# Add-residual RMSNorm: 64 KiB runs in three fixed slots, all transfers in one queue

## The chip, the cores and the metric

The kernel runs on one core of one Trainium2 chip. The metric is the device time of one execution in microseconds (us), as the median of several runs. Beside it there is one profiled execution, from which all durations of single instructions and transfers come.

## The reference

```python
def reference(x, residual, gamma, eps):
    z = x + residual
    rms = np.sqrt(np.mean(z ** 2, axis=-1, keepdims=True) + eps)
    return (z / rms * gamma).astype(np.float32)
```

The arrays x, residual and the output are 32 x 2048 x 2048 in float32, so 65,536 rows of 2,048 elements, 537 MB each. gamma has 2,048 elements. Each row is added, its mean square is taken, and the row is scaled by one number and by gamma. There is no matrix product. Each element of x and residual is read once, and each of the output is written once: 1,611 MB pass between HBM and SBUF, the memory on the core.

## The kernel before, in words

SBUF has 128 partitions. The rows are cut into 256 tiles of 256 rows; in each tile a partition holds R = 2 neighbouring rows (L29), so that its part of a transfer is one run of 16 KiB, and a transfer moves 2 MiB.

One loop (L50) runs over the tiles. For each it loads x (L53) and residual (L54) through SyncE's DMA queue (SP, queue q1 of the profile). VectorE (DVE) adds the two in place into the x tile, both rows in one instruction (L56). ScalarE (ACT) squares each row and sums it in the same instruction (L61), the squares themselves going to a scratch tile in PSUM that nobody reads; then it takes the root of mean plus eps (L69). VectorE forms the reciprocal (L77), and scales each row by it and by gamma in one instruction, again in place (L80). ScalarE's own queue then stores the x tile to the output (L89; queue q10).

What orders the work are the tile pools, from which the framework sets the waits: six buffers for x (L45) and four for residual (L46). A load of x waits until the store that used its buffer six tiles earlier has landed; a load of residual waits until the add that read its buffer has ended. Instructions of one engine, DMA issues among them, go in the order of the program, so a DMA issue that waits holds all that are behind it in the same queue.

gamma is brought to all partitions by one DMA ahead of the loop that reads its 8 KiB 128 times (L41).

Of the kernel before, what the change touches and what calls it, by code (L numbers as in the profile page):

```python
# [1 line left out]

# [4 lines left out]


@with_exitstack  # L10
def kernel(
    ctx: ExitStack,
    tc: tile.TileContext,
    x: bass.AP,
    residual: bass.AP,
    gamma: bass.AP,
    eps: float,
    out: bass.AP,
):
    nc = tc.nc  # L20
    P = nc.NUM_PARTITIONS
    fp32 = mybir.dt.float32

    x_f = x.flatten_outer_dims()
    r_f = residual.flatten_outer_dims()
    o_f = out.flatten_outer_dims()

    n_rows, D = x_f.shape
    R = 2  # L29
    assert n_rows % (P * R) == 0  # L30
    n_tiles = n_rows // (P * R)

    x_t = x_f.rearrange("(n p r) m -> n p r m", p=P, r=R)
    r_t = r_f.rearrange("(n p r) m -> n p r m", p=P, r=R)
    o_t = o_f.rearrange("(n p r) m -> n p r m", p=P, r=R)

    inv_d = 1.0 / float(D)

    singles = ctx.enter_context(tc.tile_pool(name="singles", bufs=1))
    gamma_tile = singles.tile([P, D], fp32)  # L40
    nc.sync.dma_start(out=gamma_tile, in_=gamma.partition_broadcast(P))  # L41
    eps_tile = singles.tile([P, 1], fp32)
    nc.vector.memset(eps_tile, float(eps))  # L43

    xio = ctx.enter_context(tc.tile_pool(name="xio", bufs=6))  # L45
    rio = ctx.enter_context(tc.tile_pool(name="rio", bufs=4))  # L46
    stats = ctx.enter_context(tc.tile_pool(name="stats", bufs=8))
    psum = ctx.enter_context(tc.tile_pool(name="psum", bufs=1, space=bass.MemoryType.PSUM))

    for i in range(n_tiles):  # L50
        x_tile = xio.tile([P, R, D], fp32)
        r_tile = rio.tile([P, R, D], fp32)
        nc.sync.dma_start(out=x_tile, in_=x_t[i])  # L53
        nc.sync.dma_start(out=r_tile, in_=r_t[i])  # L54

        nc.vector.tensor_add(out=x_tile, in0=x_tile, in1=r_tile)  # L56

        sq_junk = psum.tile([P, D], fp32)
        ssq = stats.tile([P, R], fp32)
        for g in range(R):  # L60
            nc.scalar.activation(  # L61
                out=sq_junk,
                in_=x_tile[:, g, :],
                func=mybir.ActivationFunctionType.Square,
                accum_out=ssq[:, g : g + 1],
            )

        rms = stats.tile([P, R], fp32)
        nc.scalar.activation(  # L69
            out=rms,  # L70
            in_=ssq,
            func=mybir.ActivationFunctionType.Sqrt,
            bias=eps_tile,
            scale=inv_d,
        )
        rstd = stats.tile([P, R], fp32)
        nc.vector.reciprocal(out=rstd, in_=rms)  # L77

        for g in range(R):
            nc.vector.scalar_tensor_tensor(  # L80
                out=x_tile[:, g, :],
                in0=x_tile[:, g, :],
                scalar=rstd[:, g : g + 1],
                in1=gamma_tile,
                op0=mybir.AluOpType.mult,
                op1=mybir.AluOpType.mult,
            )

        nc.scalar.dma_start(out=o_t[i], in_=x_tile)  # L89


# [1 line left out]
_INS = ['x', 'residual', 'gamma', 'eps']  # L93
_OUTS = [((32, 2048, 2048), 'float32')]
#: Inputs that are plain numbers.
_NUMBERS = {'eps': 9.999999974752427e-07}


# [26 lines left out]
```

## Time and profile before

| what | value |
|---|---|
| median of 10 runs | 3764.04 us (3763.73 to 3764.72) |
| the profiled execution, its own time | 3764.1 us |
| its span, first to last instruction | 3762.3 us |
| a load of x, issue to landing (median) | 34.6 us |
| a load of residual, issue to landing (median) | 37.2 us |
| a store, issue to landing (median) | 14.5 us |
| add of two rows, L56, DVE, 256 times | 4422 ns each |
| square and sum of one row, L61, ACT, 512 times | 1881 ns each, and 186 ns to read the sum out |
| root, L69, ACT, 256 times | 296 ns each |
| reciprocal, L77, DVE, 256 times | 158 ns each |
| scaling of one row, L80, DVE, 512 times | 2349 ns each |

The profile follows one execution. Each engine's busy time is a share of the span. The DMA line cuts the span into 40 slices, and each digit is the busy share of the core's 16 DMA engines in tenths; a 9 means 90% or more. A DMA is split over the 16 engines, each of which moves the runs of eight partitions one after another; a "packet" is one such run. A wait is written as "who waited, line <- what ended the wait: us in total, times, longest". The time from issue to landing of a DMA holds the time that it stood in its queue behind others.

### The profile page before, as it was taken

Reading aid. Unit: us, or ns where it says so; the run is one execution under the profiler, and the core shown is the slowest. Engines: PE = TensorE matmul, PEld = TensorE weight load, DVE = VectorE, ACT = ScalarE, POOL = GpSimd, SP = SyncE. Lnnn points to the kernel's source line nnn. Section 1 sums busy time; section 2 is a strip of 40 time slices with the busy share of each in tenths; the row PEclk is TensorE's granted clock in tenths of the full one; section 3 lists DMA queues with packets and bytes.
Section 4 is the critical chain, followed back from the end, with each engine's and each line's share of the span. In section 5 each row is a group of like instructions: output and inputs, shape, how many; then the busy total and the mean of one; then the engine's idle time right before and its main releaser. Section 6 shows DMA issues by size and latency. Waiting matters only on the chain.

```text
span 3762.3 us, 4011 instructions
## 1 busy us (share of the span) xinstructions
DVE 2322.4 (62%) x1025; ACT 1103.6 (29%) x1282; POOL 0.2 (0%) x4
## 2 busy tenths in 40 slices
DVE  5566656666566656666566655666556665566656
ACT  3232322323223232222323222222323222232322
POOL 0000000000000000000000000000000000000000
DMA  9999999999999999999999999999999999999998
GB/s 416 431 430 431 431 430 431 430 431 430 431 430 431 430 431 431 431 430 431 431 431 430 431 430 431 431 430 431 430 431 430 431 431 430 431 430 431 431 430 357
DMA packets 110767, 1611.96 MB, mean 428 GB/s; under 512 B 12304, under 2 KB 12304, under 8 KB 12304
## 3 DMA queue, kind: packets, MB, share of 16 engines
q1 hardware_dynamic: 73872, 1074.82, 66.9%
q10 hardware_dynamic: 36864, 536.89, 33.3%
q14 instruction: 31, 0.25, 0.0%
HBM read 1074.79 MB, written 536.87 MB: 428 GB/s over the span
## 4 chain that ended last, share of the span: by engine, by line
DMA 91%; DVE 8%; issue 1%; SPq 0%; ACT 0%; DVEq 0%
DMA r_tile<-in_residual_dram 53%; DMA x_tile<-in_x_dram 23%; DMA out_dram<-x_tile 15%; DVE x_tile L80 5%; DVE x_tile L56 3%; SPq L53 0%; ACT sq_junk L61 0%; DVE rstd L77 0%; DVEq L120 0%; SPq L54 0%; DVEq L56 0%; SPq L41 0%; ACT rms L69 0%
## 5 line engine op out<-in xcount | busy, mean ns | idle before, releaser
L56 DVE TENSOR_TENSOR x_tile<-x_tile,r_tile 128x4096 f32<-128x4096 f32 x256 | 1132.1, 4422 | 1412.7 <-DMA r_tile<-in_residual_dram 1412.6
L61 ACT ACTIVATE sq_junk<-x_tile 128x2048 f32<-128x2048 f32 x512 | 963.3, 1881 | 2637.8 <-DVE x_tile L56 2629.7
L80 DVE SCALAR_TENSOR_TENSOR x_tile<-x_tile,rstd,gamma_tile 128x2048 f32<-128x2048 f32 x512 | 1181.4, 2349 | 9.2
L61 ACT ACTIVATION_READ_ACCUMULATOR sq_junk<-x_tile 128x1 f32 x512 | 95.4, 186 | 0.0
L69 ACT ACTIVATE rms<-ssq,eps_tile 128x2 f32<-128x2 f32 x256 | 75.7, 296 | 8.2
L77 DVE RECIPROCAL rstd<-rms 128x2 f32<-128x2 f32 x256 | 40.5, 158 | 10.1 <-ACT rms L69 10.1
L61 ACT ACT_TABLE_LOAD x1 | 1.3, 1283 | 0.7 <-PEq L106 0.7
L69 ACT ACT_TABLE_LOAD x1 | 1.3, 1283 | 0.0
L43 DVE MEMSET eps_tile<- 128x1 f32 x1 | 0.1, 59 | 0.8 <-PEq L106 0.8
L106 POOL MEMSET const-bfloat16-1.0<- 128x1 bf16 x1 | 0.1, 101 | 0.0
L106 POOL MEMSET const-uint8-127<- 128x1 uint8 x1 | 0.1, 101 | 0.0
L106 POOL MEMSET const-float32-0.0<- 128x1 f32 x1 | 0.1, 98 | 0.2 <-issue 0.2
L106 POOL MEMSET const-float32-1.0<- 128x1 f32 x1 | 0.1, 98 | 0.0
## 6 DMA issues: line engine op xcount, KB each, us to landing
x_tile<-in_x_dram SPq DMA_DIRECT2D x256, 2048.0 KB, 34.6
r_tile<-in_residual_dram SPq DMA_DIRECT2D x256, 2048.0 KB, 37.2
out_dram<-x_tile ACTq DMA_DIRECT2D x256, 2048.0 KB, 14.5
gamma_tile<-in_gamma_dram SPq DMA_DIRECT2D x1, 1024.0 KB, 4.5
```

Source lines behind the costliest of these rows:

```text
L43: nc.vector.memset(eps_tile, float(eps))
L56: nc.vector.tensor_add(out=x_tile, in0=x_tile, in1=r_tile)
L61: nc.scalar.activation(out=sq_junk, in_=x_tile[:, g, :], func=mybir.ActivationFunctionType.Square, accum_out=ssq[:, g : g + 1],)
L69: nc.scalar.activation(out=rms, in_=ssq, func=mybir.ActivationFunctionType.Sqrt, bias=eps_tile, scale=inv_d,)
L77: nc.vector.reciprocal(out=rstd, in_=rms)
L80: nc.vector.scalar_tensor_tensor(out=x_tile[:, g, :], in0=x_tile[:, g, :], scalar=rstd[:, g : g + 1], in1=gamma_tile, op0=mybir.AluOpType. ...
L106: nc = _bacc.Bacc("TRN2", target_bir_lowering=False, num_devices=1)
```

## The change

The tile grows from 2 to 8 rows per partition: 64 tiles, each transfer 8 MiB with one run of 64 KiB per partition. The pools of x and residual are gone. In their place stand two fixed slots, z0 and z1, of eight rows for x, used in turn by even and odd tiles, and one area for residual, r_area, of nine rows. Even tiles put their residual into rows 0 to 7 of the area, odd tiles into rows 1 to 8. So the residual of an odd tile doesn't touch row 0, and that of an even tile doesn't touch row 8. The add of a tile is split to match: first the seven rows that the next residual will overwrite, then the one row that it won't.

All loads and stores go through SyncE's queue, in an order written out by hand: residual(0), x(0) in four pieces, x(1), residual(1), and then in each step store(i−1), residual(i+1), x(i+1); at the end store(last−1) and store(last) in four pieces. A store thus stands in the same queue as the loads. The first and the last tile are computed by pieces of two rows; the others by eight rows, squared in two groups of four with one root, one reciprocal instruction and four scalings each.

gamma is no longer read 128 times: four DMAs on ScalarE's queue bring it to partitions 0, 32, 64 and 96, into the ninth row of r_area, which is set to zero before, and one stream shuffle on VectorE spreads it within each group of 32 partitions into a tile in PSUM, from where the scaling reads it.

```diff
-    R = 2
+    R = 8
...
-    singles = ctx.enter_context(tc.tile_pool(name="singles", bufs=1))
-    gamma_tile = singles.tile([P, D], fp32)
-    nc.sync.dma_start(out=gamma_tile, in_=gamma.partition_broadcast(P))
...
-    xio = ctx.enter_context(tc.tile_pool(name="xio", bufs=6))
-    rio = ctx.enter_context(tc.tile_pool(name="rio", bufs=4))
...
+    z_slots = [slots.tile([P, R, D], fp32, name=f"z{k}") for k in range(2)]
+    r_area = slots.tile([P, R + 1, D], fp32, name="r_area")
...
+    sq_junk = psum.tile([P, D], fp32, name="sq_junk")
+    gamma_tile = psum.tile([P, D], fp32, name="gamma_tile")
...
+    def load_r(i):
+        a = i % 2
+        nc.sync.dma_start(out=r_area[:, a : a + R, :], in_=r_t[i])
...
+    def load_x(i, piece=R):
+        z = z_slots[i % 2]
+        for a in range(0, R, piece):
+            s = slice(a, a + piece)
+            nc.sync.dma_start(out=z[:, s, :], in_=x_t[i][:, s, :])
...
+    def store(i, piece=R):
+        z = z_slots[i % 2]
+        for a in range(0, R, piece):
+            s = slice(a, a + piece)
+            nc.sync.dma_start(out=o_t[i][:, s, :], in_=z[:, s, :])
...
+    def add(i, a, b):
+        z = z_slots[i % 2]
+        o = i % 2
+        nc.vector.tensor_add(
+            out=z[:, a:b, :], in0=z[:, a:b, :], in1=r_area[:, a + o : b + o, :]
+        )
...
+    def compute(i):
+        if i % 2 == 0:
+            order = list(range(1, R)) + [0]
+            add(i, 1, R)
+            add(i, 0, 1)
+        else:
+            order = list(range(R))
+            add(i, 0, R - 1)
+            add(i, R - 1, R)
+        groups = (order[:4], order[4:])
+        rms = [square(i, g) for g in groups]
+        for g, m in zip(groups, rms):
+            scale(i, g, m)
+
+    def compute_by_pieces(i):
+        groups = [list(range(a, a + 2)) for a in range(0, R, 2)]
+        before = None
+        for g in groups:
+            add(i, g[0], g[-1] + 1)
+            m = square(i, g)
+            if before is not None:
+                scale(i, *before)
+            before = (g, m)
+        scale(i, *before)
...
+    def load_gamma():
+        stage = r_area[:, R, :]
+        nc.vector.memset(stage, 0.0)
+        for q in range(4):
+            nc.scalar.dma_start(
+                out=r_area[32 * q : 32 * q + 1, R, :], in_=gamma.partition_broadcast(1)
             )
+        nc.vector.stream_shuffle(gamma_tile, stage, [0] * 32)
...
+    load_r(0)
+    load_x(0, 2)
+    load_gamma()
+    load_x(1)
+    compute_by_pieces(0)
+    load_r(1)
+    last = n_tiles - 1
+    for i in range(1, n_tiles):
+        store(i - 1)
+        if i < last:
+            compute(i)
+            load_r(i + 1)
+            load_x(i + 1, 2 if i + 1 == last else R)
+    compute_by_pieces(last)
+    store(last, 2)
```

The functions square and scale hold the instructions of L61 to L69 and of L77 to L80 of before, over the rows that they are given.

More of the change, by code (lines that the diff above doesn't have):

```diff
@@ L22 @@
     fp32 = mybir.dt.float32
+    Act = mybir.ActivationFunctionType
+    mult = mybir.AluOpType.mult
     x_f = x.flatten_outer_dims()
@@ L28 @@
     n_rows, D = x_f.shape
-    R = 2
+    R = 8
     assert n_rows % (P * R) == 0
     n_tiles = n_rows // (P * R)
+    assert n_tiles >= 3
     x_t = x_f.rearrange("(n p r) m -> n p r m", p=P, r=R)
@@ L37 @@
     inv_d = 1.0 / float(D)
-    singles = ctx.enter_context(tc.tile_pool(name="singles", bufs=1))
-    gamma_tile = singles.tile([P, D], fp32)
-    nc.sync.dma_start(out=gamma_tile, in_=gamma.partition_broadcast(P))
-    eps_tile = singles.tile([P, 1], fp32)
-    nc.vector.memset(eps_tile, float(eps))
-    xio = ctx.enter_context(tc.tile_pool(name="xio", bufs=6))
-    rio = ctx.enter_context(tc.tile_pool(name="rio", bufs=4))
-    stats = ctx.enter_context(tc.tile_pool(name="stats", bufs=8))
-    psum = ctx.enter_context(tc.tile_pool(name="psum", bufs=1, space=bass.MemoryType.PSUM))
@@ L50 @@
[L50 to L60, printed above, removed]
+    slots = ctx.enter_context(tc.tile_pool(name="slots", bufs=1))
+    stats = ctx.enter_context(tc.tile_pool(name="stats", bufs=4))
@@ new lines @@
+    psum = ctx.enter_context(tc.tile_pool(name="psum", bufs=1, space=bass.MemoryType.PSUM))
+    z_slots = [slots.tile([P, R, D], fp32, name=f"z{k}") for k in range(2)]
+    r_area = slots.tile([P, R + 1, D], fp32, name="r_area")
+    eps_tile = slots.tile([P, 1], fp32, name="eps_tile")
+    sq_junk = psum.tile([P, D], fp32, name="sq_junk")
+    gamma_tile = psum.tile([P, D], fp32, name="gamma_tile")
+    nc.vector.memset(eps_tile, float(eps))
+    def load_r(i):
+        a = i % 2
+        nc.sync.dma_start(out=r_area[:, a : a + R, :], in_=r_t[i])
@@ L61, with square @@
+    def square(i, rows):
+        z = z_slots[i % 2]
+        ssq = stats.tile([P, 4], fp32, name="ssq")
+        for k, g in enumerate(rows):
             nc.scalar.activation(
[L62 to L65, printed above, removed]
-            )
-        rms = stats.tile([P, R], fp32)
+                out=sq_junk, in_=z[:, g, :], func=Act.Square, accum_out=ssq[:, k : k + 1]
+            )
+        n = len(rows)
+        rms = stats.tile([P, 4], fp32, name="rms")
@@ L69, with scale @@
         nc.scalar.activation(
[L70 to L74, printed above, removed]
-        )
-        rstd = stats.tile([P, R], fp32)
-        nc.vector.reciprocal(out=rstd, in_=rms)
-        for g in range(R):
+            out=rms[:, :n], in_=ssq[:, :n], func=Act.Sqrt, bias=eps_tile, scale=inv_d
+        )
+        return rms
+    def scale(i, rows, rms):
+        z = z_slots[i % 2]
+        n = len(rows)
+        rstd = stats.tile([P, 4], fp32, name="rstd")
+        nc.vector.reciprocal(out=rstd[:, :n], in_=rms[:, :n])
+        for k, g in enumerate(rows):
@@ L80 @@
             nc.vector.scalar_tensor_tensor(
-                out=x_tile[:, g, :],
-                in0=x_tile[:, g, :],
-                scalar=rstd[:, g : g + 1],
+                out=z[:, g, :],
+                in0=z[:, g, :],
+                scalar=rstd[:, k : k + 1],
                 in1=gamma_tile,
-                op0=mybir.AluOpType.mult,
-                op1=mybir.AluOpType.mult,
-            )
-        nc.scalar.dma_start(out=o_t[i], in_=x_tile)
+                op0=mult,
+                op1=mult,
+            )
@@ new lines, in load_gamma @@
+    def load_gamma():
[4 more added lines that the diff above has]
+                out=r_area[32 * q : 32 * q + 1, R, :], in_=gamma.partition_broadcast(1)
+            )
+        nc.vector.stream_shuffle(gamma_tile, stage, [0] * 32)
[12 more added lines that the diff above has]
+            load_x(i + 1, 2 if i + 1 == last else R)
```

## The prediction

> **What bounds the kernel now.** I read the page's first two parts, then the DMA queues, then the busy time by stretches, the waits of VectorE and of the queue that issues the loads, and last the packet records of the trace (queue, start, duration and bytes of each DMA packet).
>
> ```profile
> DVE 2322.4 (62%) x1025; ACT 1103.6 (29%) x1282; POOL 0.2 (0%) x4
> ...
> DMA  9999999999999999999999999999999999999998
> ...
> DMA packets 110767, 1611.96 MB, mean 428 GB/s; under 512 B 12304, under 2 KB 12304, under 8 KB 12304
> ...
> q1 hardware_dynamic: 73872, 1074.82, 66.9%
> q10 hardware_dynamic: 36864, 536.89, 33.3%
> ```
>
> The two queues' packets fill 66.9 + 33.3 = 100.2% of 16 engines' span: the 16 DMA engines are the bound, and VectorE (62%) and ScalarE (29%) have room. The packets are 98,304 of 16 KiB (one per partition row), 128 of 8 KiB (gamma), and 12,304 of 4 bytes, which are 16 completion marks for each of 769 DMAs.
>
> ```profile
> 200.00:3600.00 3400.00, 2106.37 (x930) 997.79 (x1160) 0.00 (x0) 1.00 1.01 431
> ...
> 3720.00:3730.00 10.00, 2.28 (x1) 4.05 (x5) 0.00 (x0) 1.00 0.98 419
> 3730.00:3740.00 10.00, 9.93 (x7) 4.30 (x5) 0.00 (x0) 1.00 0.40 170
> 3740.00:3750.00 10.00, 5.92 (x2) 4.00 (x4) 0.00 (x0) 1.00 0.77 328
> 3750.00:3756.00 6.00, 4.78 (x3) 0.29 (x1) 0.00 (x0) 1.00 0.00 0
> 3756.00:3762.30 6.30, 0.00 (x0) 0.00 (x0) 0.00 (x0) 1.00 0.79 333
> ```
>
> (Stretch, its length, busy DVE, ACT, POOL, clock, DMA share, GB/s.) For 3,400 us nothing but the DMA rate counts, 431 GB/s. The tail is different: from 3730 on the engines idle 0.60 × 10 + 0.23 × 10 + 6 + 0.21 × 6.3 = 15.6 us, because the last tiles' sums run after the last load.
>
> ```profile
> DVE x_tile L56 <- DMA r_tile<-in_residual_dram: 1412.6, 131, 14.3
> ...
> SPq L53 <- DMA out_dram<-x_tile: 1603.9, 126, 16.6
> SPq L54 <- DMA x_tile<-in_x_dram: 1002.3, 127, 9.4
> ```
>
> VectorE waits for data, and the load queue for stores that free buffers: in both the DMA is last.
>
> **What the Trainium skill says.** "DMA: Bandwidth & Descriptors", section "Where 436 GB/s comes from", gives a fabric ceiling of 435.2 GB/s for the 16 engines, 27.2 GB/s each. The trace's 431 is 1% below it, so longer packets can win about 1% and no more. Section "Why small descriptors are slow (HBM only)" of the same page puts a fixed cost of about 3 cycles on each packet[...]. The records agree in kind and give 5 ns: while only loads run, one engine starts a 16 KiB packet every 607 ns and an 8 KiB packet every 306 ns, so 8 KiB of data cost 301 ns and the packet itself 306 − 301 = 5. (At a completion mark the distance is 613, so a mark costs 6.) "SBUF — State Buffer", section "Who interferes with whom", says that DMA does not contend with compute engines. The trace agrees: the add on L56 takes 4417 to 4427 ns in all 256 cases.
>
> **The change, part by part.** Sums are of the profiled execution: span 3762.3, its time 3764.1, so 1.8 lies around the span; the median of the runs shown is 3764.04, the same within 0.1.
>
> (1) *Longer runs.* 64 tiles of 8 MiB per array instead of 256 of 2 MiB. Each engine serves 8 partitions. Of 192 tile transfers, 189 go whole and 3 (first x, last x, last store) in four pieces. If a 64 KiB run is one packet it takes 4 × 602 + 5 = 2413 ns. Per engine: 189 × 8 × 2413 = 3648.5 us, 3 × 4 × 8 × 607 = 58.3 us, and 201 marks × 6 ns = 1.2 us: 3708.0 us. The same sum for before is 6144 × 607 + 768 × 6 = 3734.0. The steady stretch shows a little more: at 430.6 GB/s (records, 200 to 3600 us) a packet takes 16 × 16384 B / 430.6 GB/s = 608.7 ns, against 607 + 6/8 = 607.75. These 0.15% are irregular delays, which I keep: +5.6 us, giving 3713.6.
>
> (2) *Gamma.* The 1 MiB broadcast was 8 × 306 ns = 2.4 us per engine ahead of the first x. Now 32 KiB pass on ScalarE's queue beside the first residual load, 0.1 us. A memset and a shuffle over 128x2048 are added on VectorE. No such shuffle is in the trace; even at twice the scale row's 2.35 us it ends long before the first x piece lands (about 1.75 + 19.3 + 4.8 = 26 us), so I take nothing. If it failed to hide, it would cost at most its own few us once.
>
> (3) *Head.* The first packet starts at 1.75 us, and some 0.5 is lost while the engines come up. Kept: 2.3 us. The first tile goes by pieces: VectorE has 4.42 (add) + 4.70 (two scales) + 0.16 a piece, in the order add, add, scale, add, scale; starting at 26 and with one table load on ScalarE, the fourth add ends near 50 us. The second residual load waits for it and is needed when the first three transfers are out, 1.75 + 3 × 19.3 = 59.7. The first store waits for the last scale (65 us), needed at 79. Nothing is late.
>
> (4) *Steady order, one queue.* SP issues store(i−1), residual(i+1), x(i+1), store(i) ... and each waiting DMA holds all those behind it. Take x(i)'s landing as 0. store(i−1), already queued, keeps the engines busy to 19.3. residual(i+1) waits for the seven-row add of tile i (L78; the nine-row area spares it the eighth row). Landing to VectorE start: 0.35 to 0.47 us from mark to semaphore plus 0.1. The add over 14336 elements: 3.5 × 4.424 = 15.5 at most; with the reciprocal's 0.158 taken as fixed part, 15.1. From issue to first packet: the last store of before is issued at 3755.20 and its packets start 0.85 to 0.99 later. So residual(i+1) flows at 16.4 to 17.1, 2.2 to 2.9 us before it is needed. This slack is the cover of the whole plan, 62 times. x(i+1) waits for store(i−1) to land (20) and is needed at 38.6. store(i) waits for the scales: adds to 17.9, squares of two groups of four (2.07 each, plus 0.3) from 15.6 to 24.1 and 32.6, scales to about 43; needed at 58. Next late after the residual's wait is therefore nothing within 14 us. Cost 0.
>
> (5) *Stores unmixed.* Before, stores always ran beside loads; now all 16 engines store at once for 19.3 us. The trace shows that only in the last store: eight packets at a mean distance of 616 ns, mostly 610 to 617, once 642, against 607.8 in loads. If the 8.6 ns go with the packet they shrink to a quarter, 512 × 8.6 ns = 4.4 us; if with the bytes, 2048 × 8.6 = 17.6. Below nothing is possible too, should the irregular 5.6 us stem from mixing. I take 9 and keep −5.6 to 17.6 for the range.
>
> (6) *Tail.* The 15.6 us go: store(62) covers 19.3 us after the last x, in which VectorE works through pieces (36.8 us from 7 after the last x load begins, so to 44); counted from that start, the pieces are needed by 38.6, 43.5, 48.3, 53.1 and ready at about 21, 30, 39, 44. What remains is 1.2 us from the last packet (3761.1) to the end of the span.
>
> Sum: 3713.6 + 0.1 + 2.3 + 9 + 1.2 = 3726.2 span, + 1.8 = **3728.0 us**. Own range 3713 to 3737.
>
> **The rivals.** *A: runs are cut.* A 64 KiB run may travel as 16 KiB packets; nothing before shows a longer one. Then (1) is 6144 × 607 + 1.2 + 5.6 = 3736.2, and with the rest 3741 to 3759, about 3750: only tail, gamma and marks are won. *B: the residual waits in vain, slower.* Place: SP at residual(i+1). Price: 62 times whatever the chain add-to-load exceeds 19.3 us. Against it stand 2.2 to 2.9 us of slack; for it, that in mixed traffic a DMA's last engine completes well after its first (median 0.7 to 8.4 us by semaphore; 0.35 while only loads run). If the chain were 5 us longer than I sum, 2.4 us × 62 = 149, ending at 3877. From 3.2 us beyond my sum (0.6 us × 62 = 37) it is slower than before. *C: addresses.* "DMA: Bandwidth & Descriptors", section "Latency and other measured facts", shows 207 instead of 214 GB/s per direction at a row pitch of 512 KiB. Here neighbouring partitions move from 16 to 64 KiB apart; no run here shows such a pitch. If 3.4% were lost all along: + 126, 3854.
>
> **How the numbers follow.** Likeliest case 0.66 (3713 to 3737), A 0.16, B 0.12, C 0.06. About 0.2% (7.5 us) is what this measurement can tell from no change; A reaches inside that band with its top, some 0.03, and B can start small, 0.02. So faster 0.79, same 0.05, slower 0.16. The range takes the likeliest case and all of A's bulk: 3712 to 3757, leaving out B and C.
>
> **What would show it.** Packets: about 24,200 of 64 KiB (189 × 128), distance 2413 ns in loads; four times as many means A. DMA share full in all slices, also the last, at about 433 to 434 GB/s. VectorE's waits should name x (it now lands last); a gap of DMA between store and residual load, repeated every 58 us, means B. Distances well above 2413 inside load packets mean C, inside store packets the upper end of (5). The prediction fails if the seven-row add takes over 17 us or if loads start later than 1.5 us after issue.

## The result and the profile after

| | before | after |
|---|---|---|
| median of the runs | 3764.09 us (28 runs) | 3802.87 us (8 runs, 3798.7 to 3807.7) |
| ratio to before, 95% interval | 1 | 1.0102 (1.0093 to 1.011) |
| profiled execution: time, span | 3764.1, 3762.3 us | 3803.4, 3801.6 us |

The change makes the kernel 1.0% slower. The forecast was 3728, 1% faster, with a range up to 3757: wrong in sign, and outside its range. The span is 3801.6 − 3726.2 = 75.4 us above the sum.

The page of the changed kernel, in the same views as before:

```profile
DVE 2296.2 (60%) x780; ACT 1060.1 (28%) x1158; POOL 0.2 (0%) x4
...
DMA  9999999999999999999999999999999999999999
...
DMA packets 28972, 1610.82 MB, mean 424 GB/s; under 512 B 3220, under 2 KB 3220, under 8 KB 3220
...
q1 hardware_dynamic: 28944, 1610.63, 99.7%
q10 hardware_dynamic: 8, 0.03, 0.0%
```

The DMA engines are still the bound, and one queue's packets fill 99.7% of their span, now with a 9 in the last slice too. The packets are what was planned: 28,972 less 3,220 marks, 1,536 of 16 KiB, 4 of gamma and 20 instruction fetches leaves 24,192 of 64 KiB. So runs aren't cut, and rival A is out. Yet the mean rate fell from 428 to 424 GB/s. A queue that is 99.7% "full" doesn't say that its packets are fast: a packet that takes longer fills the same share.

The stretches of the changed kernel (stretch, its length, busy DVE, ACT, POOL, clock, DMA share, GB/s):

```profile
200.00:3600.00 3400.00, 2056.93 (x686) 941.61 (x1027) 0.00 (x0) 1.00 1.00 424
...
3770.00:3780.00 10.00, 10.00 (x7) 3.37 (x5) 0.00 (x0) 1.00 0.92 396
3780.00:3790.00 10.00, 2.79 (x2) 0.00 (x0) 0.00 (x0) 1.00 1.01 431
3790.00:3801.60 11.60, 0.00 (x0) 0.00 (x0) 0.00 (x0) 1.00 0.77 327
```

The tail is repaired as forecast: no stretch at 0, no long idling. The loss lies in the steady stretch. One tile is three transfers of 8.39 MB, 25.17 MB together, which at 424 GB/s take 59.4 us; 24 packets of the forecast 2413 ns take 57.9. About 1.4 us are lost per tile, 62 times.

The packet records of the trace say how. The median 64 KiB packet takes 2418 ns, as summed, but the mean is 2467 and the longest 4513. Each engine moves eight packets of every transfer; by place among the eight, the first of a residual load averages about 2800 ns and the last of an x load about 3150, and the others 2418 to 2445. These two places are on either side of the store: the order in the queue is x, store, residual. Over all packets, the time beyond the median is 74.9 us per engine. Idle gaps between packets are only 12.5 us per engine. Together they are 87 us, the 1.4 us of each tile.

Where does the queue stand at that place? The waits of the queue that issues the DMAs, in the changed kernel (us in total, times, longest), and one such place in its timeline (start, duration, engine and line, operation):

```profile
SPq L61 <- DVE z L78: 1983.8, 63, 32.4
SPq L73 <- DVE z L102: 1429.8, 66, 22.6
SPq L67 <- DMA out_dram<-z: 237.5, 62, 4.6
```

```profile
1016.62 0.34 SPq L73 DMA_DIRECT2D out_dram<-z  x1
1034.12 17.29 DVE L78 TENSOR_TENSOR z<-z,r_area 128x14336 f32<-128x14336 f32 x2 [17.53 <-DMA z<-in_x_dram]
1049.24 0.33 SPq L61 DMA_DIRECT2D r_area<-in_residual_dram  x1
...
1053.36 0.33 SPq L67 DMA_DIRECT2D z<-in_x_dram  x1
```

The add starts at 1034.12, its first instruction (seven rows) ends 15.1 us later, and the residual load is issued at 1049.24. Its first packet starts at 1050.30 in the records, 1.06 us after the issue. The 16 engines did not end together, however: their last x packets ended from 1030.84 to 1033.67, a spread of 2.8 us. The add waits for the slowest. The two fastest engines finish the store at 1050.16 and 1050.28, before the residual is there, and four more by 1050.38; the slowest three finish it at 1052.4 to 1053.0 and change over without loss. The slack of 2.2 to 2.9 us had been counted on the slowest engine alone: for it 2.7 us are measured, for the fastest none.

This fits the Trainium skill, "DMA: Bandwidth & Descriptors", section "Why a DMA increments its semaphore by 16 and not by 1": the engines of one DMA finish independently, and only the full count says that all data has landed. The trace agrees: the wait ended at 1034.12, after the last engine's 1033.67, not after the first one's 1030.84.

### The profile page after: what moved, and what is told of

Same layout as the page of the kernel before. It is cut to its first block, busy times and chain, and to the rows that moved or that the text cites. A ratio compares the mean times of both kernels' runs of the same rounds, so it can differ in the third digit from the quotient of the medians.

```text
span 3801.6 us, 2509 instructions
## 1 busy us (share of the span) xinstructions
DVE 2296.2 (60%) x780; ACT 1060.1 (28%) x1158; POOL 0.2 (0%) x4
## 2 busy tenths in 40 slices
DMA packets 28972, 1610.82 MB, mean 424 GB/s; under 512 B 3220, under 2 KB 3220, under 8 KB 3220
## 3 DMA queue, kind: packets, MB, share of 16 engines
q1 hardware_dynamic: 28944, 1610.63, 99.7%
## 4 chain that ended last, share of the span: by engine, by line
DMA 64%; DVE 29%; ACT 7%; issue 0%; DVEq 0%; SPq 0%
DMA z<-in_x_dram 33%; DMA out_dram<-z 30%; DVE z L102 15%; DVE z L78 13%; ACT sq_junk L86 7%; DMA r_area<-in_residual_dram 1%; ACT rms L91 0%; DVE rstd L100 0%; DVEq L191 0%; ACT L91 0%; DVEq L78 0%; SPq L61 0%; SPq L67 0%
## 5 line engine op out<-in xcount | busy, mean ns | idle before, releaser
L78 DVE TENSOR_TENSOR z<-z,r_area 128x14336 f32<-128x14336 f32 (+2 forms) x132 | 1107.5, 8430 | 1068.3 <-DMA z<-in_x_dram 1051.2
L86 ACT ACTIVATE sq_junk<-z 128x2048 f32<-128x2048 f32 x512 | 962.0, 1879 | 2704.6 <-DVE z L78 2692.6
L102 DVE SCALAR_TENSOR_TENSOR z<-z,rstd,gamma_tile 128x2048 f32<-128x2048 f32 x512 | 1167.9, 2344 | 4.5
L100 DVE RECIPROCAL rstd<-rms 128x4 f32<-128x4 f32 (+1 forms) x132 | 22.7, 173 | 391.3 <-ACT rms L91 391.3
L86 ACT ACTIVATION_READ_ACCUMULATOR sq_junk<-z 128x1 f32 x512 | 95.3, 186 | 0.0
L91 ACT ACTIVATE rms<-ssq,eps_tile 128x4 f32<-128x4 f32 (+1 forms) x132 | 39.2, 297 | 4.3
```

The source lines that it names most:

```text
L78: nc.vector.tensor_add(out=z[:, a:b, :], in0=z[:, a:b, :], in1=r_area[:, a + o : b + o, :])
L86: nc.scalar.activation(out=sq_junk, in_=z[:, g, :], func=Act.Square, accum_out=ssq[:, k : k + 1])
L91: nc.scalar.activation(out=rms[:, :n], in_=ssq[:, :n], func=Act.Sqrt, bias=eps_tile, scale=inv_d)
L100: nc.vector.reciprocal(out=rstd[:, :n], in_=rms[:, :n])
L102: nc.vector.scalar_tensor_tensor(out=z[:, g, :], in0=z[:, g, :], scalar=rstd[:, k : k + 1], in1=gamma_tile, op0=mult, op1=mult,)
```

## The experiments

Theories. **S**: the residual load is released with too little slack; engines run dry (have no packet to move) and then lose time at the changes around the store. Rivals, with their letters in the expectations: **L** long packets themselves, **P** the 64 KiB pitch (rival C of the forecast), **M** mixing of directions in one stream, **O** the change of direction in one queue, **Q** only that something stands behind the store in the queue. S2 and R came with the last four runs. In this table, worked out from the packet records, "slow packets" is the time that the packets of one engine took beyond the median of their size, and "gaps" the time in which it had none; both are means over the 16 engines.

| kernel | median us | ratio (95%) | span | slow packets | gaps |
|---|---|---|---|---|---|
| after | 3802.87 | 1.0102 (1.0093–1.011) | 3801.6 | 74.9 | 12.5 |
| a1_runs16 | 3831.08 | 1.0166 (1.0141–1.019) | 3830.6 | 77.7 | 12.8 |
| a2_runs16_pitch16 | 3814.31 | 1.0134 (1.0119–1.0149) | 3817.9 | 65.6 | 12.4 |
| a3_no_release | 3725.79 | 0.9898 (0.9883–0.9913) | 3724.0 | 4.3 | 0.35 |
| a4_store_actq | 3975.45 | 1.0544 (1.0508–1.058) | 3971.9 | 120.7 | 138 |
| b1_six_rows | 3740.31 | 0.9935 (0.9921–0.995) | 3737.2 | 20.2 | 1.25 |
| b2_eight_rows | 3983.03 | 1.0579 (1.0562–1.0597) | 3980.5 | 118.7 | 146 |
| c1_split_r | 3730.94 | 0.991 (0.9895–0.9925) | 3729.3 | 6.3 | 0.54 |
| c2_split_r_runs16 | 3764.85 | 1.0001 (0.9992–1.001) | 3763.2 | 9.5 | 5.8 |
| e1_hold_late | 3729.89 | 0.9908 (0.9891–0.9924) | 3728.2 | 6.2 | 0.49 |
| e2_hold_early | 3729.53 | 0.9907 (0.9893–0.9922) | 3727.9 | 6.2 | 0.45 |
| e3_hold_at_x | 3959.86 | 1.0516 (1.05–1.0532) | 3959.0 | 121.4 | 118.9 |
| e4_hold_at_x_longer | 3967.58 | 1.054 (1.0523–1.0558) | 3961.4 | 122.3 | 121.8 |

### Is it the length of the runs, or their pitch?

a1_runs16 makes every transfer in four DMAs of two rows, so runs are 16 KiB again; a2_runs16_pitch16 also lays neighbouring partitions 16 KiB apart.

```diff
-        nc.sync.dma_start(out=r_area[:, a : a + R, :], in_=r_t[i])
+        for a in range(0, R, 2):
+            nc.sync.dma_start(out=r_area[:, a + o : a + o + 2, :], in_=r_t[i][:, a : a + 2, :])
...
+    x_t = x_f.rearrange("(n p r) m -> n p r m", p=P, r=R)           (a1; a2 in its place:)
+    x_t = x_f.rearrange("(n g p r) m -> n p g r m", p=P, g=4, r=2)
```

> The changed kernel with every transfer cut into four DMAs of two rows per partition: runs of 16 KiB, neighbouring partitions still 64 KiB apart, same order, same queue. Theory L (long packets are what suffers at each change between loads and stores): the slow load packets vanish, 16 KiB loads keep about 607 ns, and the time is 3736 + 5 = about 3742 us. Theory M (loads suffer whenever other engines store, whatever their length) and theory P (the 64 KiB pitch is at fault): the loss of 1.2 us per tile stays, about 3742 + 75 = 3817 us. Theory S (too little slack at the residual's release): also about 3817.

> As the kernel with runs of 16 KiB, but each piece's rows lie so that neighbouring partitions are 16 KiB apart, as in the kernel before. Theory P (pitch): about 3742 us here while the one with the 64 KiB pitch stays at 3817. Theory L: about 3742 in both. Theory M or S: about 3817 in both.

Measured 3831.08, 14 us above the rivals' figure, and 3814.31. a1's steady stretch:

```profile
200.00:3600.00 3400.00, 2045.68 (x685) 940.70 (x1026) 0.00 (x0) 1.00 1.00 421
```

With short runs the loss stays: 77.7 us of slow packets against 74.9, and a median 16 KiB packet as fast as ever (611 ns). So L is rejected, and with the pitch of before it stays too, so P, the forecast's rival C, is rejected as the cause. Whether pitch has a small part is open: a2 ends 17 us below a1 and loses 12 us less to slow packets, but a1's own runs lie 20 us apart.

### Is it the release of the residual load?

a3_no_release lets the add read x twice, so nothing reads the residual, and no residual load waits for an add. The residual is left out of the sum, so this kernel computes something else; every transfer and instruction is still there.

```diff
-            out=z[:, a:b, :], in0=z[:, a:b, :], in1=r_area[:, a + o : b + o, :]
+            out=z[:, a:b, :], in0=z[:, a:b, :], in1=z[:, a:b, :]
```

> The changed kernel with the add reading x twice instead of x and residual, so that the residual is left out of the sum and its loads wait for no add. Theory S (the residual load comes just too late, engines idle and drift apart): the slow packets and gaps go, about 3727 us. Theories L, M, P: the slow load packets at the changes stay, no lower than about 3790 us.

Measured 3725.79, as S expects. Its steady stretch and the waits of its queue:

```profile
200.00:3600.00 3400.00, 2102.14 (x703) 973.68 (x1062) 0.00 (x0) 1.00 1.00 434
```

```profile
SPq L67 <- DMA out_dram<-z: 2118.7, 62, 38.7
SPq L73 <- DVE z L102: 1436.5, 66, 39.1
```

The line "SPq L61 <- DVE z L78" is gone, and the rate is 434 GB/s, that of the sum. The same queue, the same order, the same long runs and the same unmixed stores thus run at full rate: M falls, and O as a cost of every change falls with it. The books close: (74.9 − 4.3) + (12.5 − 0.35) = 82.7 us less per engine, from which go 5.3 us because a3's engines end further apart (its slowest 6.1 us after the mean, after's 0.8). That is 77.4; the spans differ by 77.6.

### How much slack is needed?

b1_six_rows releases the residual after six rows (the residual is left out of the other two), 2.2 us earlier than the change; b2_eight_rows after all eight, 2.1 us later. Both keep the residual in rows 0 to 7.

```diff
-            add(i, 1, R)
-            add(i, 0, 1)
+        add(i, 0, 6)                                                 (b1)
+        nc.vector.tensor_add(out=z[:, 6:R, :], in0=z[:, 6:R, :], in1=z[:, 6:R, :])
...
+        add(i, 0, R)                                                 (b2)
```

> The changed kernel with the residual left out of two of the eight rows in all tiles but the first and last: the next residual load waits for an add of six rows, so it comes 2.2 us earlier than in the changed kernel. Theory S (the release comes when the fastest engines have run dry; that both restarts them and keeps them in step, so that all change from load to store at once): nearly all of the 76 us go, 3725 to 3740 us. Theory Q (a load packet is slow when nothing but the store is queued behind it, whatever the slack): the part at the change from load to store stays, 3726 + 62 x 0.8 = about 3775 us.

> The changed kernel without the ninth row's use: every residual lies in rows 0 to 7, one add of eight rows, so the next residual load comes 2.1 us later. Theory S: the whole 2.1 us of each tile are added as a gap or as slow packets, 3803 + 62 x 2.1 = about 3933 us. If only part of the engines waits at the seven-row release, less, not under 3850.

Measured 3740.31, just above what S says, and 3983.03, 50 us more than expected. The steady stretch of b1 with one of its adds and the next residual load, then the same of b2:

```profile
200.00:3600.00 3400.00, 2094.03 (x698) 963.71 (x1051) 0.00 (x0) 1.00 1.00 432
...
1017.25 12.96 DVE L77 TENSOR_TENSOR z<-z,r_area 128x12288 f32<-128x12288 f32 x1 [18.19 <-DMA z<-in_x_dram]
...
1030.23 0.33 SPq L60 DMA_DIRECT2D r_area<-in_residual_dram  x1
```

```profile
200.00:3600.00 3400.00, 1954.32 (x600) 906.75 (x988) 0.00 (x0) 1.00 0.96 404
...
1013.30 17.23 DVE L77 TENSOR_TENSOR z<-z,r_area 128x16384 f32<-128x16384 f32 x1 [17.66 <-DMA z<-in_x_dram]
1030.55 0.33 SPq L60 DMA_DIRECT2D r_area<-in_residual_dram  x1
```

The residual load is issued 13.0 us (b1) and 17.25 us (b2) after its add began, where the change needs 15.1. Against a3's span: +13.2 (b1), +77.6 (after), +256.5 us (b2). Moving the release by 2.2 us costs 64 us over 62 tiles, 47% of 62 × 2.2; by a further 2.1 us, 179, or 137% of 62 × 2.1. A price of "gap × 62" therefore isn't enough, as the table shows: beside b2's gaps of 146 us stand 118.7 us of slow packets.

### A kernel that keeps the computation and gives the slack

c1_split_r loads the residual in two halves of four rows and cuts the add alike. The first half is released after four rows instead of seven, three row adds earlier; the ninth row is no longer needed for it.

```diff
-        nc.sync.dma_start(out=r_area[:, a : a + R, :], in_=r_t[i])
+        for a in range(0, R, 4):
+            nc.sync.dma_start(out=r_area[:, a : a + 4, :], in_=r_t[i][:, a : a + 4, :])
...
-            add(i, 0, R - 1)
-            add(i, R - 1, R)
+        add(i, 0, 4)
+        add(i, 4, R)
```

> The changed kernel with each residual transfer cut in two of four rows (runs of 32 KiB) and the add cut the same way, no ninth row: the first half is released after four rows, 6.5 us earlier, the second half at about the time of before but needed 9.7 us later. Theory S: about 3726 + 3 = 3729 us, below the kernel before. Theory Q: 3729 + 62 x 0.8 = about 3779 us.

Measured **3730.94 us, 0.991 of before** (0.9895 to 0.9925): it beats both kernels. Its steady stretch and its end, then a place of its timeline:

```profile
200.00:3600.00 3400.00, 2099.40 (x705) 980.43 (x1062) 0.00 (x0) 1.00 1.00 433
...
3710.00:3720.00 10.00, 1.14 (x1) 0.00 (x0) 0.00 (x0) 1.00 0.99 424
3720.00:3729.30 9.30, 0.00 (x0) 0.00 (x0) 0.00 (x0) 1.00 0.17 71
```

```profile
1014.24 17.30 DVE L78 TENSOR_TENSOR z<-z,r_area 128x8192 f32<-128x8192 f32 x2 [22.36 <-DMA z<-in_x_dram]
1022.96 8.93 SPq L61 DMA_DIRECT2D r_area<-in_residual_dram  x2
...
1033.49 0.33 SPq L67 DMA_DIRECT2D z<-in_x_dram  x1
...
1050.06 0.34 SPq L73 DMA_DIRECT2D out_dram<-z  x1
```

The first half is issued 8.7 us after the add began, where the change needed 15.1. In this tile the engines end the store from 1029.1 to 1033.0 in the records, and the residual, with the 1.0 us from issue to first packet, is there at 1024.0: 5.1 us of slack even for the fastest engine. The residual still waits for an add and still stands behind the store, so Q is rejected: only the slack differs. The last line of the stretches shows what remains: in the last 9.3 us only 17% of the engines' time is used, since one or a few engines end late.

c2_split_r_runs16 is c1 with all transfers in pieces of two rows, so 16 KiB runs.

> The kernel with the residual's release after four rows, and all transfers in pieces of two rows, runs of 16 KiB. It differs from the one with long runs in the packet length alone. Theory of the sum (5 ns per packet, 6 ns per mark): 4608 packets more x 5 ns and 560 marks more x 6 ns per engine, so about 25 us above the one with long runs: about 3752 us. If long runs bring nothing: equal to it.

Measured 3764.85, the same as before. Its steady stretch and its end:

```profile
200.00:3600.00 3400.00, 2071.74 (x696) 963.39 (x1044) 0.00 (x0) 1.00 1.01 430
...
3750.00:3757.00 7.00, 0.00 (x0) 0.00 (x0) 0.00 (x0) 1.00 0.24 101
3757.00:3763.20 6.20, 0.00 (x0) 0.00 (x0) 0.00 (x0) 1.00 0.04 18
```

Fifteen of its 16 engines end at 3751.5 to 3751.9, where the expectation had the kernel end; one ends at 3761.7. Why that one lags is open. The expectation counts too many packets: c2 has 4,024 more per engine than c1 and 503 more marks, which at its prices is 23 us. The median is 33.9 us above c1's, but not all of that is the length of the runs. By the mean end of the 16 engines it is 30.6 us; 3.2 of them are more slow packets and 5.2 more gaps (near 3737 us, 13 of 16 engines have no packet for 4.4 to 7.0 us, until the next piece of the last tile is ready to be stored). Some 22 us are left for the packets and marks themselves, near the 23.

### Another queue for the store

a4_store_actq issues the stores on ScalarE's queue.

```diff
-            nc.sync.dma_start(out=o_t[i][:, s, :], in_=z[:, s, :])
+            nc.scalar.dma_start(out=o_t[i][:, s, :], in_=z[:, s, :])
```

> The changed kernel with the stores issued on ScalarE's queue, so that they start when a tile is ready and run packet by packet beside the loads. Theory O (a change of direction within one queue is what costs): the slow packets go; if the waits leave no gap, about 3730 us. Theories M and P: more packets are mixed, so at least 3802 us, and up to 3752 x 1.3 if every mixed 64 KiB load takes 3.1 us. Theory L: as M.

Measured 3975.45. The wait that grew in its queue:

```profile
SPq L67 <- DMA out_dram<-z: 3533.4, 62, 61.5
```

The x load waits for the landing of a store that now runs beside the residual load and lands later. The engines then run dry, 138 us each. A new wait covers what was to be measured, so this run decides nothing about O.

### Does running dry elsewhere do the same?

The last four start from c1 and make x(i+1) wait for something late in tile i, so that the engines run dry, if at all, between two *loads*. R says that only the change between store and load loses; S2 says that running dry anywhere unsettles the engines, and that the changes then cost again.

```diff
+        nc.vector.memset(z_slots[(i + 1) % 2][:, 0, 0:1], 0.0)       (e1 after the scalings, e2 between the two groups)
...
+        nc.vector.tensor_copy(                                       (e3 with w = 1, e4 with w = 1024; after the scalings)
+            out=z_slots[(i + 1) % 2][:, 0, 0:w], in_=z_slots[i % 2][:, R - 1, D - w : D]
+        )
```

> The kernel with the split residual (3731 us, no late release), in which each whole x load waits in addition for a one-element memset that VectorE does after the tile's last scaling, about 36.3 us after the previous x has landed. The slowest engine needs x at 38.7 and the packets start 0.9 after issue, so that engine keeps 1.4 us of slack, but an engine that is more than 1.4 us ahead is held, between two loads. Theory S as it stands now, with two parts (engines held in step change from load to store at once and lose about 0.8 us a tile there; engines that run dry lose 0.4 more at the restart): 3731 + 62 x 0.8 = about 3781 us, up to 3805 with the restarts. Theory R (only running dry between store and load costs, the place of the hold matters): no more than 3740.

> The same one-element memset and the same added wait, but between the two groups of scalings, about 27 us after the previous x has landed, so that engines up to 10 us ahead are not held. Both theories: about 3731 us, the wait as such costs nothing.

> The kernel with the split residual, in which each whole x load waits in addition for a one-element copy that reads the last row scaled, so that it can't be moved ahead of the scalings: x is issued 36.4 us after the previous x has landed. Its packets start at 37.3, and the slowest engine needs them at 38.7; engines more than 1.4 us ahead run dry, between residual and x, so between two loads. Theory S2 (engines settle into an order in which the change from load to store is free, and running dry anywhere in the cycle undoes it): 3731 + 62 x 0.5 to 1.1 = 3762 to 3800 us, with slow load packets at the change to the store. Theory R (only running dry between store and load does harm): no more than 3740.

> The same with a copy of 1,024 elements, some 0.5 to 1.1 us longer, so that x's packets start 0.3 to 0.9 us before the slowest engine needs them. Theory S2: as the one-element copy, or up to 30 us more. Theory R: as the one-element copy, no more than 3745.

e2: 3729.53; the added wait by itself costs nothing. e1: 3729.89, but it missed its aim. Its timeline:

```profile
1013.80 17.29 DVE L78 TENSOR_TENSOR z<-z,r_area 128x8192 f32<-128x8192 f32 x2 [22.34 <-DMA z<-in_x_dram]
...
1040.37 0.06 DVE L119 MEMSET z<- 128x1 f32 x1
1040.48 0.33 SPq L67 DMA_DIRECT2D z<-in_x_dram  x1
```

The memset depends on no scaling and was moved ahead of the second group, so x is issued 26.7 us after the add began instead of 36. e1 became a second e2 and decides nothing. e3 ties it to the last scaling by its data; its timeline and stretch:

```profile
1004.39 17.29 DVE L78 TENSOR_TENSOR z<-z,r_area 128x8192 f32<-128x8192 f32 x2 [25.94 <-DMA z<-in_x_dram]
...
1040.21 0.15 DVE L119 COPY z<-z 128x1 f32<-128x1 f32 x1
1040.39 0.33 SPq L67 DMA_DIRECT2D z<-in_x_dram  x1
```

```profile
200.00:3600.00 3400.00, 1972.73 (x715) 913.97 (x990) 0.00 (x0) 1.00 0.97 407
```

Now x is issued 36.0 us after the add began, and the kernel takes 3959.86 (e4, with a copy of 1024 elements: 3967.58). R is rejected. What rejects it is the 121.4 us of slow packets, which S2 expects and R doesn't; the gaps lengthen the kernel under any theory. The size is far over what S2 expected, since engines ran dry for 118.9 us each, about 1.9 us per tile. The records show why that is more than the few that the expectation had in mind: in most tiles of e3 fifteen engines end x within some 0.6 us, and one a further 2.2 us later (medians); the add waits for that one, and the fifteen are held. In e3 the first packet of x takes 3.1 us on average, and the last x packet ahead of the store 3.6.

What the changes lose, from the packet records, in us, as means over the 16 engines: "into the store" is the time beyond the median of the packets that start from 10 us before to 6 us after a store's first packet, "out of it" the same from 13 to 28 us after it. Changes are numbered from 0.

| kernel | into the store: first change | next three | mean of 1–19 | out of it, mean of 1–19 |
|---|---|---|---|---|
| a3 | 0.62 | 0.31, 0.07, 0.03 | 0.06 | 0 |
| c1 | 1.02 | 0.02, 0.05, 0.04 | 0.04 | 0.01 |
| e2 | 0.74 | 0.22, 0.05, 0.13 | 0.05 | 0 |
| b1 | 0.76 | 0.17, 0.33, 0.61 | 0.26 | 0.07 |
| after | 0.83 | 0.98, 0.80, 0.64 | 0.85 | 0.41 |
| b2 | 0.83 | 1.09, 1.12, 0.83 | 1.03 | 0.77 |
| e3 | 0.82 | 0.20, 1.06, 1.60 | 1.17 | 0.01 |

Every kernel of the table loses 0.6 to 1.0 us at its first change from loads to a store. Kernels whose engines always have a next packet (a3, c1, e2) lose next to nothing after a few changes: they settle. Where some engines run dry in each tile, the loss returns in each tile. For the changed kernel the means over all 62 changes are 0.76 and 0.41, so 62 × 1.17 = 73 us of the 74.9.

## Why the prediction was wrong

The step that failed is **(4)**: "This slack is the cover of the whole plan, 62 times … Cost 0." Its chain was right in its terms (add 15.1 us, issue to first packet 1.06 where 0.85 to 0.99 was taken), so neither of the two conditions occurred under which it said that it fails (an add over 17 us, loads later than 1.5 us after issue). The slack it was set against was wrong. It took the landing of x, which is the slowest engine's, as the moment at which all engines begin the store, so that all would end it 19.3 us later. In the changed kernel the engines end x 1.5 to 3.0 us apart (median 2.55) and the store likewise, as much as the whole slack, and nearly all of its 12.5 us of gaps stand where the fastest then wait for the residual. In a3, where no residual load waits for an add, the engines end a store 5.0 us apart (median; 2.8 to 8.0). The add waits for the slowest engine, while the fastest needs the residual first. The 62 places cost some 75 us of slow packets and 12.5 of gaps instead of 0. a3 shows it by taking the wait away (77.6 us of span return), c1 by giving it slack.

**Rival B** named the right place and sign but a wrong price: 62 times the excess of the chain over 19.3 us, slower only "from 3.2 us beyond my sum". The chain was not longer at all. The larger part of the loss is no gap but slow packets at the changes, which nothing in the profile of before showed. The forecast's own test, "a gap of DMA between store and residual load, repeated every 58 us", would have found only a seventh of it, and slow load packets had been named as a sign of C, which a2 rejects.

**(1)** held: 24,192 packets, at a distance of 2414 ns (forecast 2413). With c1 against c2, the longer runs are a real gain, some 22 us. **(2)** held, but narrowly: the shuffle takes 2.3 us and the memset 1.8 on VectorE, while it waits for data. It was to end long before the first x piece lands; but gamma's four small DMAs, issued from 3.06 us on, landed at 24.4, and the shuffle ended at 26.75, 2.1 us before the first add. **(3)** held: a3's gaps are 0.35 us per engine in all, the head's included. **(5)** was mis-sized: 0 instead of 9 us. In the stores of a3 an engine starts a packet every 2415 ns on average, in its loads every 2417 to 2418. **(6)** held for the 15.6 us, but the sum left out that engines end apart: a3's from 3714.7 to 3722.6. These 6 us took the place of the 9 in (5), so that a3's 3725.79 stands near the forecast's 3728.0 partly by two errors that cancel.

Rivals A (packet count) and C (a1, a2) were rightly held unlikely. 0.12 for B was too little: a slack of 2.2 to 2.9 us needed 62 times, which the prediction itself set beside a spread of 0.7 to 8.4 us in mixed traffic, was no cover.

Open: why an engine that has run dry is slow at the following changes. How far the engines are apart doesn't explain it alone: at the second change from x to a store, c1's engines end x 2.7 us apart and lose 0.02 us, the changed kernel's 2.6 us apart and lose 0.98. Also open are c2's lagging engine, and a4's part about one queue or two.

## What to carry to other kernels

Count slack from the fastest DMA engine at the end of the one transfer to the slowest at the end of the other, not from one landing: here 2.2 to 2.9 us against the slowest end was none against the fastest, while c1 has 5.1 us even against the fastest in the tile shown. If a load of a single-buffered area is released late, split the load and what reads it, so that its first part can be queued early; here that left 5 us against a3, which has no such wait, and turned +1.0% into −0.9%. A full DMA share doesn't show full speed: compare GB/s, and the packets' mean with their median.

## What the runs showed of the hardware that was not expected

- The first change from loads to a store on all engines costs 0.6 to 1.0 us in every kernel of the table, and later ones 0.04 to 0.06 on average where no engine runs dry (c1, a3, e2).
- Where engines run dry, packets at the changes are slow: 64 KiB of x took 3.1 us on average at the start and 3.6 ahead of the store in e3, against 2.42.
- One queue in which loads and stores take turns moves 434 GB/s (a3), with the engines a median 5.0 us apart; a load packet and a store packet start nearly equally far apart (2417 to 2418 ns and 2415).
- The changed kernel varies by 9 us from run to run, and so do others that lose at the changes (b2 10, e3 12, a1 20); a3, c1, e1 and e2 vary by 0.5 to 1.2.
